# Down products of 768 tokens by a 2x2 recursion of seven, and attention values taken a turn later

## The chip, the cores and the metric

The kernel runs on one core of one Trainium2 chip. The metric is device microseconds from start to end of one execution, median of several. A second number, the span, is what the profiler saw from the first to the last instruction of one profiled execution. The engines are called PE (TensorE; its weight load is listed as PEld), DVE (VectorE), ACT (ScalarE), POOL (GpSimd) and SP (SyncE). SP and POOL issue most DMAs.

## The reference

One layer of a gated hybrid decoder for 1024 prompt tokens and 8 sample tokens (1032 in all), model width 1024, feed-forward width 2816 (22 blocks of 128):

```python
z = x @ w_in
a_out = rg_lru(conv4(xr)) * gelu(yr)                # branch a
s_out = sliding_window_attention(q, k, v, sinks)    # branch s: window 128, 16 heads, 4 kv heads, head_dim 64
c_out = mem_attn(xq, mem_k, mem_v)                  # branch c: 256 memory tokens
merged = sum(gates[:, :, n] * (br @ w_branch[n]) for n, br in enumerate((a_out, s_out, c_out)))
h = layer_norm(ALPHA * x + merged @ w_out, ln1_g, ln1_b)
gt, up = jnp.split(h @ w_gate_up, 2, axis=-1)
h = layer_norm(ALPHA * h + (jax.nn.silu(gt) * up) @ w_down, ln2_g, ln2_b)
```

Outputs are h for both groups, the new recurrent states and the new key and value caches; for the sample group the window cache moves by one position (copies named o_swk and o_swv).

## The kernel before, in words

Tensors lie transposed: features on the 128 partitions, tokens along the columns. Every fp32 product is made of three matmuls in a rounded type (mm3): each operand is split into a high part (a cast on ACT, line 81) and a low part (source minus high part, on DVE, line 82), and the product is high x high, high x low and low x high, summed in one PSUM bank. So each operand tile costs one ACT and one DVE operation, and each product needs both before its three matmuls can run.

Stages in order of time: the input projection (up to about 690 us), memory attention with parts of branches a and c (to 830), local attention (`windows`, 830 to 1040) with branch products between its steps, branch s and the output projection (to 1217), gate and up (to 1677), down with the second layer norm (to 1933), and the end of the last layer norm.

**Local attention.** 4 kv heads x 8 blocks of 128 tokens give 32 turns. A turn makes scores and a softmax for one block (`win_scores`: PE scores L590 and L591, DVE L594, ACT L598), then fills with branch matmuls (`fill(1)`), then finishes the block of the turn before (`win_values`: PE transposes L615 into a bank bt, ACT and DVE split it into bph and bpl, PE multiplies both with the values into a bank bo, L620 and L621).

**Gate and up.** 20 of the 22 blocks are units f = 2 to 21; gate and up of one block are products of 1024-wide rows made by a 2x2 recursion: seven products i = 0 to 6 in place of eight, over halves of the features and halves of the tokens. One unit step (f, i) is 24 matmuls of 258 columns (two column parts p). `fast_quarter` makes the weight operand of a step three steps ahead (a sum of weight quarters for i = 1, 2, 4, 5, then the split, u..h and u..l). After the products, DVE and ACT put the results together (za, zb, ft) and SP stores the silu(gt) * up row of the block to a DRAM scratch scr_f. In units 6 and 12, SP also copies a whole cache of 1 MB from DRAM to DRAM.

**Down.** `down` takes three chunks of tokens (CH: 384, 384, 264). Per chunk 22 rows are loaded by POOL from scr_f (L1260) and split (gh, gl), and for each of eight output blocks m, the weights are loaded by SP in pieces of up to 512 columns and split (wd_h, wd_l), so every weight piece is loaded and split three times over the stage; L1251 to L1253 are the three matmuls. The result of a block is added to the residual (L1307) and to a running sum (L1311). The layer norm of a chunk is a generator whose steps are taken between the products of the next chunk; the last chunk ends with a form of its own (`last_layer_norm`).

**Order.** The order on each engine is the order in which the code is written, as a recording layer puts it down with priorities; `issue_after` pins an operation behind a named one. Tiles come from pools; a pool opened after another has closed takes its room, and a tile waits for the last user of that room.

```python
def split(self, hi, lo, src):
    ins = self.nc.scalar.copy(hi, src).ins
    self.nc.vector.tensor_sub(lo, src, hi.bitcast(F32))
    return ins
```

## Time and profile before

| what | us |
|---|---|
| runs before, median of 3 | 1946.44 |
| lowest, highest | 1943.93, 1948.19 |
| time of the profiled execution | 1948.63 |
| its span | 1946.9 |
| mean granted TensorE clock | 0.996 |
| gate and up, main stretch | 1216.8 to 1655.0 |
| down, first to last matmul | 1677.7 to 1932.6 |

Rows of the views by stage give for each engine the busy time in a stretch and, in brackets, the instructions counted there. A granted clock of 1.00 means that TensorE was never slowed there. In rows of waits, the columns are the total time waited, how often, and the longest; the engine is named first, then what it wanted to write and at which line, and behind the arrow what it waited for. In groups by line, `out<-in` names the tiles, the shape is partitions x columns, and `319` is the mean duration in ns.

### The profile page before, as it was taken

The page shows a single profiled execution, that of the slowest core. Times are in us where ns is not written, and L with a number is a line of the kernel's source. Part 1 is how long each engine was busy: PE and PEld are TensorE (multiplying, and loading weights), DVE is VectorE, ACT ScalarE, POOL GpSimd, SP SyncE. Part 2 cuts the span into 40 slices and gives each one's busy share as a digit, 9 for nine tenths or more (in the row PEclk, how much of TensorE's full clock was granted, in tenths as well). Part 3 has the DMA queues.
Part 4 walks back from the last instruction along what each step waited for, and adds up shares of the span by engine and source line. Part 5 has one row for each costly group of instructions (what it writes and reads, how often), then busy time and mean ns, then how long its engine had stood idle before and what let it go on. Part 6 is the DMA issues. An engine that isn't in the chain of part 4 may idle for free. (4 is left out here: it accounts for less than half of the span.)

```text
span 1946.9 us, 37967 instructions
## 1 busy us (share of the span) xinstructions
PE 1912.7 (98%) x14356; PEld 1883.0 (97%) x14356; DVE 1363.5 (70%) x2875; ACT 1012.9 (52%) x2198; POOL 133.8 (7%) x218
## 2 busy tenths in 40 slices
PE   8999999999999999999999999999999999999997
PEld 8999999999999989989999999999999999999997
DVE  8678887888777645389877557975565656747566
ACT  5465565455556545388775245643333333635444
POOL 1000000000010200011110000000000000402002
PEclk9999999999999999999999999999999999999999
DMA  7444545465323866567525341122222222846554
GB/s 231 146 160 148 174 166 184 128 215 168 130 90 134 287 206 222 153 170 218 161 77 171 99 145 46 39 78 97 78 88 87 90 80 78 280 130 186 158 155 138
DMA packets 170919, 281.92 MB, mean 145 GB/s; under 512 B 20864, under 2 KB 85456, under 8 KB 170704
## 3 DMA queue, kind: packets, MB, share of 16 engines
q1 hardware_dynamic: 165840, 264.72, 43.2%
q0 software_dynamic: 4896, 14.78, 2.3%
q8 instruction: 112, 1.84, 0.4%
q14 instruction: 71, 0.58, 0.1%
HBM read 214.64 MB, written 66.85 MB: 145 GB/s over the span
## 5 line engine op out<-in xcount | busy, mean ns | idle before, releaser
L1253 PE MATMUL dl<-gh,wd_l 128*128 128x384 f32 (+1 forms) x528 | 168.5, 319 | 3.1 <-DVE wd_l L82 3.1
L1251 PE MATMUL dl<-gh,wd_h 128*128 128x384 f32 (+1 forms) x528 | 168.0, 319 | 1.1 <-ACT gh L81 1.1
L1252 PE MATMUL dl<-gl,wd_h 128*128 128x384 f32 (+1 forms) x528 | 168.2, 319 | 0.0
L1253 PEld LDWEIGHTS dl<-gh,wd_l 128*128 128x128 f32 x528 | 99.9, 189 | 3.5 <-DVE wd_l L82 3.5
L1251 PEld LDWEIGHTS dl<-gh,wd_h 128*128 128x128 f32 x528 | 99.9, 189 | 1.3 <-ACT gh L81 1.3
L1252 PEld LDWEIGHTS dl<-gl,wd_h 128*128 128x128 f32 x528 | 99.9, 189 | 0.5 <-DVE gl L82 0.5
L1260 POOL DMA_DIRECT2D gl<-scr_f x66 | 35.5, 539 | 789.0 <-PE fb L1186 630.6
L81 ACT CAST u_1h<-us 128x512 fp32r<-128x512 f32 x48 | 29.8, 621 | 87.2 <-issue 43.5
L598 ACT ACTIVATE bp<-bp,bst 128x257 f32<-128x257 f32 (+1 forms) x128 | 62.8, 493 | 18.1 <-DVE bst L594 18.0
L287 DVE TENSOR_TENSOR us<-ur,ur 128x512 f32<-128x512 f32 x96 | 66.0, 688 | 5.1 <-DMA ur<-win 3.1
L81 ACT CAST u_2h<-us 128x512 fp32r<-128x512 f32 x48 | 29.7, 619 | 76.6 <-PE fb L1186 38.2
L287 DVE TENSOR_TENSOR us<-us,ur 128x512 f32<-128x512 f32 x96 | 66.2, 689 | 2.3
L82 DVE TENSOR_TENSOR u_6l<-ur,u_6h 128x512 fp32r<-128x512 f32 x48 | 33.9, 706 | 44.9 <-PE fb L1187 28.9
L115 PE MATMUL brs<-bsH,wbs_h 128*128 128x384 f32 (+1 forms) x192 | 61.1, 319 | 1.0 <-ACT bsH L81 1.0
L82 DVE TENSOR_TENSOR u_4l<-us,u_4h 128x512 fp32r<-128x512 f32 x48 | 33.0, 688 | 40.1 <-PE fb L1187 29.1
L117 PE MATMUL brs<-bsH,wbs_l 128*128 128x384 f32 (+1 forms) x192 | 61.0, 318 | 0.0
L116 PE MATMUL brs<-bsL,wbs_h 128*128 128x384 f32 (+1 forms) x192 | 61.0, 318 | 0.0
L594 DVE CUSTOM_DVE_ANT_0 bp<-bs,mask,nsnk 128x256 f32<-128x256 f32 (+1 forms) x128 | 54.6, 458 | 3.2 <-PE bs L591 2.2
L82 DVE TENSOR_TENSOR u_5l<-us,u_5h 128x512 fp32r<-128x512 f32 x48 | 33.1, 689 | 30.0 <-PE fd L1187 14.9
L1205 ACT ACTIVATE ft<-za 128x516 f32<-128x516 f32 x40 | 25.5, 636 | 52.4 <-DVE za L1204 52.4
L81 ACT CAST u_5h<-us 128x512 fp32r<-128x512 f32 x48 | 30.0, 624 | 38.2 <-DVE us L287 24.9
L81 ACT CAST u_0h<-ur 128x512 fp32r<-128x512 f32 x48 | 29.8, 621 | 38.5 <-PE ub L304 19.1
(2019 smaller groups left out, 8111.4 us busy)
## 6 DMA issues: line engine op xcount, KB each, us to landing
ur<-win SPq DMA_DIRECT2D x112, 256.0 KB
ur<-wgu SPq DMA_DIRECT2D x80, 256.0 KB
scr_f<-ft SPq DMA_DIRECT2D x40, 258.0 KB
gl<-scr_f POOLq DMA_DIRECT2D x44, 192.0 KB, 4.3
dck<-cmk SPq DMA_DIRECT2D x32, 256.0 KB
dcv<-cmvT SPq DMA_DIRECT2D x32, 256.0 KB
st<-scr_q SPq DMA_DIRECT2D x32, 256.0 KB
scr_g<-za SPq DMA_DIRECT2D x10, 516.0 KB
```

What stands on the lines that cost most here:

```text
L81: ins = self.nc.scalar.copy(hi, src).ins
L82: self.nc.vector.tensor_sub(lo, src, hi.bitcast(F32))
L115: nc.tensor.matmul(ps, sh, mh, start=i == 0, stop=False)
L116: nc.tensor.matmul(ps, sh, ml, start=False, stop=False)
L117: self.last_mm = nc.tensor.matmul(ps, sl, mh, start=False, stop=closes and i == last).ins
L287: nc.vector.tensor_add(src, a, b)
L594: nc.vector.tensor_tensor_reduce(pg[g], s[:, u * 256:u * 256 + n], msk, 1.0, snk[:, g:g + 1], ALU.add, ALU.min, st[:, g:g + 1])
L598: nc.scalar.activation(x, x, AF.Exp, bias=st[:, g:g + 1], scale=-1.0, accum_out=st[:, 4 + g:5 + g])
L1251: nc.tensor.matmul(ps, sh, mh, start=k == 0, stop=False)
L1252: nc.tensor.matmul(ps, sh, ml, start=False, stop=False)
L1253: self.last_mm = nc.tensor.matmul(ps, sl, mh, start=False, stop=closes and k == NF - 1).ins
L1260: self.nc.gpsimd.dma_start(lo.bitcast(F32), self.scf[f][:, t0:t0 + n])
```

## The change

**Down.** The first 384 columns of each token half (768 tokens) go through the same recursion that gate and up use: seven products over halves of the 22 blocks (KD = 11), halves of the output blocks and the two token sides, taken in the order 0, 3, 2, 1, 5, 4, 6. A product is 4 output pairs j x 11 blocks k x 3 matmuls of 384 columns. The remaining 264 tokens (132 of each half) are taken the plain way at the end. Products 1, 2, 4 and 5 need sums of weight quarters, products 1, 2, 4 and 6 sums of row quarters.

**Where the sums are made.** 16 weight jobs in gate and up: POOL loads four pieces, four DVE additions, POOL stores four results to a DRAM scratch scr_w. Row sums per k: POOL loads two rows (two more are at hand), four DVE operations, four stores to scr_s; the last k comes in down (`last_sums`). The scratch tiles of both (pool xs) are four rooms.

**Kept lows.** The low parts of the weights of products 0, 3 and 6 stay in SBUF (wk tiles), so that three quarters of the weight pieces of the last 264 tokens need only the cast on ACT.

**Other parts.** The end of unit 21 (`unit_end`) is held until after down's first weights. The two 1 MB cache copies become sixteen. The halves of the tokens are now interleaved quarters, and a unit's row is stored in one contiguous piece. The layer norm of one token side lies in product 6, that of the other in the last part. In `windows` the transposes with their split (`win_turn`) and the value products (`win_values`) are separate, and the values of a block come one turn later, not before the sixth matmul of the branch product that fills the turn (`self.mark`). Widths of the chunks change from 384, 384, 264 to 384, 390, 258.

Local attention on PE, around the scores of block 3 of kv head 1 (bt are transposes, bs scores, bo values, bra and brc branch products). Before:

```order
L117 MATMUL bra7_2_11920<-H0_7h_8918,wba71_l_11762 128x264
L615 MATMUL bt1_1_0_11947<-ident_63,bp1_1_11823 128x128 x4
L615 MATMUL bt1_1_1_11958<-ident_63,bp1_1_11823 128x128 x4
L590 MATMUL bs1_3_0_11980<-ks1_0_11442,st1_0_11448 128x256
L591 MATMUL bs1_3_0_11980<-ks1_1_11443,st1_0_11448 128x256
L590 MATMUL bs1_3_0_11980<-ks1_0_11442,st1_1_11451 128x256
L591 MATMUL bs1_3_0_11980<-ks1_1_11443,st1_1_11451 128x256
L620 MATMUL bo1_1_11946<-bph1_1_0_11952,vs1_11460 128x512
L590 MATMUL bs1_3_1_11987<-ks1_0_11442,st1_2_11454 128x256
```

and now:

```order
L128 MATMUL bra7_2_11924<-H0_7h_8933,wba71_l_11764 128x258
L639 MATMUL bo1_0_11950<-bph1_0_0_11894,vs1_11462 128x512
L640 MATMUL bo1_0_11950<-bpl1_0_0_11895,vs1_11462 128x512
L626 MATMUL bt1_1_0_11961<-ident_63,bp1_1_11825 128x128 x4
L626 MATMUL bt1_1_1_11970<-ident_63,bp1_1_11825 128x128 x4
L601 MATMUL bs1_3_0_11982<-ks1_0_11444,st1_0_11450 128x256
L602 MATMUL bs1_3_0_11982<-ks1_1_11445,st1_0_11450 128x256
L601 MATMUL bs1_3_0_11982<-ks1_0_11444,st1_1_11453 128x256
```

The values of block 1 stood four score matmuls behind their own transposes; now the values of block 0 stand there, whose transposes were a turn earlier, ahead of the branch product.

DVE where the units end and down begins (ft21 is the last unit's row, gl the low part of a row of down, wd or wk the low part of weights). Before:

```order
L1206 SCALAR_TENSOR_TENSOR ft21_1_21655<-ft21_1_21655,za21_1_21654 128x516
L1209 SCALAR_TENSOR_TENSOR ft21_0_21639<-fb21_0_21521,ft21_0_21639 128x258
L1207 TENSOR_TENSOR ft21_1_21655<-ft21_1_21655,zb21_1_21683 128x258
L1209 SCALAR_TENSOR_TENSOR ft21_1_21655<-fb21_1_21536,ft21_1_21655 128x258
L82 TENSOR_TENSOR wd0_1_00_l_22008<-wd0_1_0r0__22005,wd0_1_00_h_22007 128x512
L82 TENSOR_TENSOR gl0_0_21840<-gl0_0_21840,gh0_0_21839 128x384
L82 TENSOR_TENSOR gl1_0_21845<-gl1_0_21845,gh1_0_21844 128x384
```

and now:

```order
L91 TENSOR_TENSOR gl0_7_22289<-gl0_7_22289,gh0_7_22288 128x384
L91 TENSOR_TENSOR wk0_1_0_22314<-wd0_1_0r_22311,wd0_1_0h_22313 128x512
L91 TENSOR_TENSOR wk0_1_1_22320<-wd0_1_1r_22317,wd0_1_1h_22319 128x512
L91 TENSOR_TENSOR wk0_1_2_22326<-wd0_1_2r_22323,wd0_1_2h_22325 128x384
L1236 SCALAR_TENSOR_TENSOR ft21_0_22071<-ft21_0_22071,za21_0_22070 128x516
L1236 SCALAR_TENSOR_TENSOR ft21_1_22087<-ft21_1_22087,za21_1_22086 128x516
L1237 TENSOR_TENSOR ft21_0_22071<-ft21_0_22071,zb21_0_22101 128x258
L1237 TENSOR_TENSOR ft21_1_22087<-ft21_1_22087,zb21_1_22115 128x258
L1239 SCALAR_TENSOR_TENSOR ft21_0_22071<-fb21_0_21945,ft21_0_22071 128x258
L1239 SCALAR_TENSOR_TENSOR ft21_1_22087<-fb21_1_21960,ft21_1_22087 128x258
L91 TENSOR_TENSOR gl0_8_22342<-gl0_8_22342,gh0_8_22341 128x384
```

The end of the last unit stood ahead of all row lows; now it stands behind eight of them and the lows of the second weights, ahead of the ninth row.

The diff, cut to its core (functions that vanish whole, `streamed` and `rows`, and the loaders of rows and weights are left out):

```diff
+CH = ((0, 384), (384, 390), (774, 258))
+CW = 390
-EARLY, EARLY_ROWS = ("mm", "s", "mm", "s"), 12
+KD = NF // 2
+NA = 384
+NC = T // 2 - NA
+DOWN_ORDER = (0, 3, 2, 1, 5, 4, 6)
+DOWN_PIECES = ((0, 4), (4, 4), (8, 3))
+SUM_PIECES = ((0, 3), (3, 3), (6, 3), (9, 2))
+KEPT = (0, 3, 6)
+EARLY = 4
+SUM_AT = {1: 0, 2: 1, 4: 2, 5: 3}
+ROW_AT = {1: 0, 4: 1, 2: 2, 6: 3}
...
+            if i == 2:
+                self.mark = self.last_mm
...
+    def win_turn(self, kv, ops, b, pg):
+
         nc = self.nc
-        nk, vs = len(range(max(b - 1, 0), b + 1)), ops[2]
-        ov = self.bank("o", f"bo{kv}_{b}")
-        for kk in range(nk):
+        out = []
+        for kk in range(2 if b else 1):
             pt = self.bank("t", f"bt{kv}_{b}_{kk}")
             for g in range(4):
                 nc.tensor.transpose(pt[:, g * P:(g + 1) * P], pg[g][:, kk * P:(kk + 1) * P], self.ident)
             hi = self.ph.tile([P, 512], F32R, tag="pt", name=f"bph{kv}_{b}_{kk}", bufs=4)
             lo = self.ph.tile([P, 512], F32R, tag="pt", name=f"bpl{kv}_{b}_{kk}", bufs=4)
             self.split(hi, lo, pt)
-            v = vs[:, max(b - 1, 0) + kk, :]
-            nc.tensor.matmul(ov, v, hi, start=kk == 0, stop=False)
-            self.last_mm = nc.tensor.matmul(ov, v, lo, start=False, stop=kk == nk - 1).ins
+            out.append((hi, lo))
+        return kv, ops[2], b, out
+
+    def win_values(self, kv, vs, b, pp):
+        nc = self.nc
+        ov = self.bank("o", f"bo{kv}_{b}")
+        with self.tc.issue_after(self.mark):
+            for kk, (hi, lo) in enumerate(pp):
+                v = vs[:, max(b - 1, 0) + kk, :]
+                nc.tensor.matmul(ov, v, hi, start=kk == 0, stop=False)
+                nc.tensor.matmul(ov, v, lo, start=False, stop=kk == len(pp) - 1)
...
-        nxt, last = self.win_load(0), None
+        nxt, last, turned = self.win_load(0), None, None
         fill(2)
         for kv in range(4):
             ops = nxt
                 pg = self.win_scores(kv, ops, b)
                 if last:
                     fill(1)
-                    self.win_values(*last)
+                if turned:
+                    self.win_values(*turned)
+                turned = last and self.win_turn(*last)
                 last = kv, ops, b, pg
                 if b == 4 and kv < 3:
                     nxt = self.win_load(kv + 1)
         fill(1)
-        self.win_values(*last)
+        self.win_values(*turned)
+        self.win_values(*self.win_turn(*last))
...
+            elif self.held is None:
+                self.unit_end(st, i, p, f, za, t, b, d)
             else:
+                self.held.append(partial(self.unit_end, st, i, p, f, za, t, b, d))
+
+    def unit_end(self, st, i, p, f, za, t, b, d):
+        nc, lo_, hi_ = self.nc, slice(0, QN), slice(QN, HT)
+        if i == 5:
+            nc.vector.tensor_add(za[:, hi_], d, st["s", 2, p])
+            nc.scalar.activation(t, za, AF.Tanh, scale=0.5)
+            nc.vector.scalar_tensor_tensor(t, t, 1.0, za, op0=ALU.add, op1=ALU.mult)
+            nc.vector.tensor_mul(t[:, hi_], t[:, hi_], st["zb", p])
+        else:
+            nc.vector.scalar_tensor_tensor(t[:, lo_], b, -0.5, t[:, lo_], op0=ALU.mult, op1=ALU.mult)
+            nc.sync.dma_start(self.scf[f][:, p * HT:(p + 1) * HT], t)
+
...
+    def scratch(self, name, n):
+        return self.xs.tile([P, NA], F32, tag="xs", name=name, bufs=4)[:, :n]
+
+    def sum_load(self, j, e):
+
+        o, n = SUM_PIECES[e][0] * P, SUM_PIECES[e][1] * P
+        raw = [self.scratch(f"dw{j}{e}{x}", n) for x in range(4)]
+        for x, a in enumerate(raw):
+            at = (x % 2) * KD * P + o
+            self.nc.gpsimd.dma_start(a, self.io["wdn"][2 * j + x // 2][:, at:at + n])
+        return j, o, n, raw
+
+    def sum_weights(self, j, o, n, raw):
+
+        nc, (a11, a12, a21, a22) = self.nc, raw
+        with self.tc.issue_after(self.last_mm):
+            nc.vector.tensor_add(a22, a21, a22)
+            nc.vector.tensor_add(a21, a11, a21)
+            nc.vector.tensor_add(a11, a22, a11)
+            nc.vector.tensor_add(a12, a11, a12)
+        for i, a in ((1, a22), (4, a21), (2, a11), (5, a12)):
+            nc.gpsimd.dma_start(self.scw[j][:, SUM_AT[i], o:o + n], a)
+
+    def row_load(self, k):
+        x = [self.scratch(f"rx{k}{h}", NA) for h in range(2)]
+        for h in range(2):
+            self.nc.gpsimd.dma_start(x[h], self.scf[k][:, h * HT:h * HT + NA])
+        return x
+
+    def row_sums(self, k, x00, x01, x10, x11, t1, t4, queue):
+
+        nc = self.nc
+        nc.vector.tensor_sub(t1, x00, x01)
+        nc.vector.tensor_sub(x01, x11, x01)
+        nc.vector.scalar_tensor_tensor(x00, x01, -1.0, x00, op0=ALU.mult, op1=ALU.subtract)
+        nc.vector.scalar_tensor_tensor(t4, x00, -1.0, x10, op0=ALU.mult, op1=ALU.subtract)
+        for i, a in ((1, t1), (4, x01), (2, x00), (6, t4)):
+            queue.dma_start(self.scs[k][:, ROW_AT[i] * NA:(ROW_AT[i] + 1) * NA], a)
...
+        jobs = deque((j, e) for j in range(KT // 2) for e in range(len(SUM_PIECES)))
...
-            if (f, i) in ((6, 2), (12, 2)):
-                name, cache = ("o_swk", "cwk") if f == 6 else ("o_swv", "cwv")
+            if i == 2 and f > 3 and caches:
+                name, cache, b = caches.popleft()
                 with self.tc.issue_after(self.last_load):
-                    self.nc.sync.dma_start(io[name][:, 0:P - 1, :], io[cache][:, 1:P, :])
+                    self.nc.sync.dma_start(io[name][b, 0:P - 1, :], io[cache][b, 1:P, :])
             if n + ahead < len(todo):
                 v, j = todo[n + ahead]
                 self.fast_quarter(st[v], j)
+            if (f, i) == (NF - 1, 5):
+                self.held = []
             self.unit_step(st[f], i)
+            if n % 4 == 0 and jobs:
+                job = self.sum_load(*jobs.popleft())
+            elif n % 4 == 3 and job:
+                self.sum_weights(*job)
+                job = None
+            if i == 3 and KD <= f < NF - 1:
+                early = self.row_load(f - KD)
+            if i == 1 and turn:
+                with self.tc.issue_after(self.last_mm):
+                    self.row_sums(*turn, self.nc.sync if f == NF - 1 else self.nc.gpsimd)
+                turn = None
             if i == 6:
+                if KD <= f < NF - 1:
+                    k = f - KD
+                    turn = (k, *early, *(st[f]["t", p][:, :NA] for p in range(2)),
+                            *(self.scratch(f"rs{k}{x}", NA) for x in range(2)))
                 del st[f]
...
+    def down_begin(self):
+        self.norm, self.lows = None, {}
+        self.rooms()
+        first = partial(self.down_row, DOWN_ORDER[0])
+        self.first_rows = [first(k, "a") for k in range(8)]
+        self.first_weights = {(DOWN_ORDER[0], 0, e): self.down_weights(DOWN_ORDER[0], 0, e) for e in range(3)}
+        with self.tc.issue_after(self.row_cast):
+            self.first_weights.update({(DOWN_ORDER[0], 1, e): self.down_weights(DOWN_ORDER[0], 1, e) for e in range(3)})
+            for held in self.held:
+                held()
+        self.first_rows += [first(k, "a") for k in range(8, KD)]
...
+        for n, i in enumerate(DOWN_ORDER):
+            ahead = deque(range(KD))
+            nxt = [None] * KD
+            for j in range(KT // 2):
+                opens = i in (0, 1, 3)
+                if opens:
+                    tag = ("mm", "mm", "mm", "o")[j] if i == 0 else "st"[j % 2]
+                    banks["b" if i == 0 else "c", j] = self.bank(tag, f"dl{i}_{j}")[:, :NA]
+                ps = banks["b" if i in (0, 2, 4, 6) else "c", j]
+                mm = partial(nc.tensor.matmul, ps, skip_group_check=not opens)
+                for e, (k0, nk) in enumerate(DOWN_PIECES):
+                    wh, wl = self.weights_of(i, j, e)
+                    for k in range(k0, k0 + nk):
+                        w = slice((k - k0) * P, (k - k0 + 1) * P)
+                        xh, xl = act[k]
+                        mm(wh[:, w], xh, start=opens and k == 0, stop=False)
+                        mm(wh[:, w], xl, start=False, stop=False)
+                        self.last_mm = mm(wl[:, w], xh, start=False, stop=k == KD - 1).ins
+                    if ahead:
+                        k = ahead.popleft()
+                        if i == 6:
+                            last[k] = self.last_row(k)
+                        else:
+                            nxt[k] = self.down_row(DOWN_ORDER[n + 1], k, "ba"[n % 2])
+                    if i == 6 and (j, e) in ((2, 0), (2, 2), (3, 1)):
+                        self.norm_step()
+                evict(i, j, ps)
+            act = nxt
+            if i == 0:
+                self.last_sums()
+            if i == 4:
+                norm_of(1)
+        for f in range(KD, NF):
+            last[f] = self.last_row(f)
...
+        for m in range(EARLY):
+            open_[m] = self.bank(("mm", "s")[m % 2], f"dc{m}")[:, :2 * NC]
+            half(m, 0, open_[m], False)
+            self.norm_step()
+            if m == EARLY - 2:
+                norm_of(0)
```

More of the change, by code (lines that the diff above doesn't have):

```diff
@@ L1314, in build @@
+        tail = lambda a: a.rearrange("p (q n) -> p q n", q=2)
+        rows = [tail(a)[:, :, NA:] for a in self.accs]
+        self.last_layer_norm(2 * NC, rows, product, V_G2, emit_to(lambda m: tail(io["o_y"][:, m, :])[:, :, NA:]), tail)
     def build(self):
@@ L1341, in build @@
                         held()
+                self.held = None
             self.sums = 2
```

263 lines of the change are left out of this document (159 added, 104 removed).

## The prediction

> **What bounds the kernel now.** The page's first part comes first: one engine fills the span.
>
> ```profile
> span 1946.9 us, 37967 instructions
> PE 1912.7 (98%) x14356; PEld 1883.0 (97%) x14356; DVE 1363.5 (70%) x2875; ACT 1012.9 (52%) x2198; POOL 133.8 (7%) x218
> PE 13%; DVE 0%; ACT 0%; issue 0%; ACTq 0%; DVEq 0%
> ```
>
> PE is busy for 98%, and the chain that ended last (third line) is followed back through PE for 13% of the span, which is the whole down stage. So time goes away only where matmuls go away or where PE stands still. Second view: busy time by stage (columns: stretch, length, then PE, PEld, DVE, ACT, POOL, granted clock, DMA share, GB/s).
>
> ```profile
> 1216.80:1655.00 438.20, 436.93 (x3644) 436.36 (x3643) 288.14 (x550) 180.81 (x365) 0.00 (x0) 1.00 0.25 80
> 1655.00:1677.60 22.60, 21.61 (x181) 21.40 (x179) 13.00 (x26) 8.91 (x19) 11.36 (x21) 1.00 0.83 265
> 1703.50:1752.20 48.70, 48.70 (x283) 48.70 (x282) 23.25 (x41) 15.29 (x27) 0.00 (x0) 1.00 0.47 130
> 1677.66:1862.20 184.54, 184.54 (x1062) 184.04 (x1063) 115.39 (x216) 90.55 (x181) 24.19 (x45) 1.00 0.59 177
> 1862.20:1932.60 70.40, 67.35 (x539) 66.72 (x539) 50.83 (x92) 36.87 (x71) 5.85 (x6) 0.98 0.54 160
> 1932.60:1946.90 14.30, 2.33 (x13) 1.66 (x11) 7.60 (x14) 5.69 (x12) 3.91 (x5) 0.71 0.22 76
> 830.00:1040.00 210.00, 207.20 (x1337) 191.77 (x1337) 175.26 (x541) 162.50 (x488) 37.58 (x61) 1.00 0.53 148
> ```
>
> Gate and up (1216.8 to 1677.6) runs a matmul of 258 columns every 436.36/3643 = 0.120 us; PE hardly waits, DVE has 34% of the time free and ACT 59%. In down the undisturbed stretch 1703.5 to 1752.2 gives one of 384 columns each 48.70/283 = 0.172 us. Local attention (830 to 1040) is tighter: DVE 83%, ACT 77%. Third view: what PE's weight load waits for in local attention, then what its matmuls wait for in the whole run.
>
> ```profile
> PEld bo L620 <- ACT bph L81: 7.0, 25, 0.5
> PEld bo L620 <- PE bra L116: 0.7, 1, 0.7
> PEld bo L620 <- issue: 0.5, 2, 0.3
> PE dl L1253 <- DVE wd_l L82: 3.1, 2, 2.2
> PE fb L1187 <- DVE u_0l L82: 1.3, 2, 0.6
> PE dl L1251 <- ACT gh L81: 1.1, 1, 1.1
> ```
>
> Value matmuls lose 8.2 us to the cast of the probabilities just transposed; down loses 1.1 us at its start and 3.1 us near its end; the units lose 1.3 us in two places.
>
> **The change, part by part.** The sum is made on the profiled execution, 1948.6 us around its span of 1946.9; the median of the runs is 1946.4, 2.2 lower, and that is taken off at the end.
>
> *Fewer matmuls: -22.7.* For 768 tokens the plain product takes 2 x 8 x 22 x 3 = 1056 matmuls of 384 columns, the recursion 7 x 4 x 11 x 3 = 924. 132 x 0.172 = 22.7 us. The other 264 tokens stay 528 matmuls. Chunks of 390 and 258 columns in place of 384 and 264 keep the columns of the earlier stages the same: nothing.
>
> *Values a turn later: -7.5.* The value matmuls now stand behind a whole fill of branch matmuls, and their operands were cast a turn before, so the 8.2 us lose their cause. What is left is how much of it comes back as a wait of the scores or transposes, on engines at 83% and 77%. Bounds: 0, all of it comes back, and -10, if smaller waits around it go too. I stay near the row, -7.5.
>
> *Cache copies: -1.3.* Two copies of 1 MB were queued ahead of a unit's weights; the two waits for u_0l are 1.3 us, the longest 0.6. Sixteen small copies, each in another unit, should leave none. Bounds -1.3 and 0.
>
> *The sums in the units: 0.* 16 weight jobs of four adds and 11 row jobs of four operations (one in down) are about 108 DVE instructions. The nearest rows are the 384-wide ones:
>
> ```profile
> L82 DVE TENSOR_TENSOR gl<-gl,gh 128x384 fp32r<-128x384 f32 x44 | 21.9, 555 | 2.6 <-ACT gh L81 2.6
> L1307 DVE SCALAR_TENSOR_TENSOR acc<-acc,dl 128x384 f32<-128x384 f32 x16 | 8.8, 552 | 4.3 <-PE dl L1253 4.3
> L981 DVE RECIPROCAL n2rs<-n2rs 128x384 f32<-128x384 f32 x2 | 5.1, 2554 | 0.7 <-ACT n2rs L978 0.7
> L1206 DVE SCALAR_TENSOR_TENSOR ft<-ft,za 128x516 f32<-128x516 f32 x3 | 2.1, 694 | 0.7 <-ACT ft L1205 0.7
> L1209 DVE SCALAR_TENSOR_TENSOR ft<-fb,ft 128x258 f32<-128x258 f32 x4 | 1.7, 425 | 0.0
> L82 DVE TENSOR_TENSOR gl<-gl,gh 128x264 fp32r<-128x264 f32 x22 | 8.8, 429 | 3.4 <-ACT gh L81 3.3
> L287 DVE TENSOR_TENSOR us<-ur,ur 128x512 f32<-128x512 f32 x96 | 66.0, 688 | 5.1 <-DMA ur<-win 3.1
> ```
>
> 104 x 0.55 = 57 us in a stage with 150 us of free DVE: 66% becomes 79%. What hides them is PE's own pace; uncovered they would cost 57 us, and the place where cover can fail is the third rival. The units' traffic, 80 GB/s, grows by some 11.5 MB of weight loads, 3.9 MB of row loads and 19 MB of stores in 438 us, to about 160 GB/s; the stretch before down ran at 265.
>
> *Units into down: +4.7.* In the new order DVE does, after the unit's last sums, three weight lows, eight row lows (gl0_0 to gl0_7), then three lows of the next weights (wk0_1, 2 x 0.69 + 0.555 = 1.9 us), then the held end of unit 21 (2 x 0.694 + 2 x 0.42 + 2 x 0.425 = 3.1 us), and only then gl0_8. PE goes through 24 matmuls on gl0_0 to gl0_7 for the first quarter and eight on the second before it needs gl0_8: about 32 x 0.172 = 5.5 us. From DVE's first row low, gl0_8 is ready after 9 x 0.555 + 1.9 + 3.1 = 10.0 us, and PE starts some 0.5 us after that low. So PE stands still for 9.5 - 5.4 = about 4.2 us. After such a stop the clock drops, as two places show, each behind a PE gap (the 2.2 us of the wd_l row above, and 1.8 us at 716):
>
> ```profile
> 716.00:721.00 5.00, 4.79 (x23) 4.79 (x24) 1.48 (x4) 1.02 (x4) 0.54 (x3) 0.66 0.46 139
> 1880.00:1885.00 5.00, 4.23 (x22) 4.23 (x23) 4.03 (x8) 1.01 (x3) 0.00 (x0) 0.66 0.56 159
> PEld dss L887 <- POOL dsk L884: 1.8, 1, 1.8
> ```
>
> A granted clock of 0.66 over 5 us is 3.4 us at half speed: 1.7 us of work lost. Together 5.9, less the 1.1 to 1.3 that the old start lost: +4.7. Bounds 0 (the rows land so late that the held work fits in before them) and +8 (the rows land at intervals and gl0_8's own landing comes on top).
>
> The Trainium skill, "TensorE: Matmul & The Clock Gate", Part 1, says that the clock falls to half after at least one idle window of about 3.4 us. The two gaps above are shorter and were followed by a half-speed window all the same, so here the measurement decides. By the page the 4.2 us stop would still pay, but a stop of 2 us would not: its sum would be up to 1.7 us lower if my stop is overestimated.
>
> *The steady products: 0.* One product takes PE 132 x 0.172 = 22.7 us. DVE does twelve weight lows (8 x 0.69 + 4 x 0.555 = 7.7), eleven row lows (6.1), four evictions (2.2) and at most four running sums (2.2): 18.2 us. POOL issues eleven row loads, SP twelve weight loads: 2.1 MB + 2.9 MB in 22.7 us, 220 GB/s, where 265 was reached.
>
> *The last part: 0.* 528 x 0.120 x 264/258 = 65 us of PE against 70.4 in the row above, so the old one lost some 5 us (3.1 of wd_l, and a slow window). The new one has weight lows for a quarter of its pieces only (the others are kept), but two layer norms instead of one now lie in the last product and in it, each with a reciprocal of 2.55 us in front of weight lows that PE waits for. I put stalls of 4 to 6 us there: 0, with bounds -4 and +2. The tail of 14.3 us has the same operations.
>
> Sum: -22.7 - 7.5 - 1.3 + 0 + 4.7 + 0 + 0 = -26.8; 1948.6 - 26.8 = 1921.8 on the profiled scale, less 2.2: **1919.5 us**.
>
> **The rivals.**
>
> *DVE becomes the bound in down.* For it: the first product has, beside 18.2, the last row sums (2.2), its own eleven row lows (6.1) and the held work (3.1), less 1.9 done before it starts: 27.7 us against 22.7; product 6 has weight lows 7.7, eleven row lows of 0.43, evictions 4.4 and a norm of 8 x 0.55 + 7 x 0.55 + 2.55 + 8 x 0.61 + 1.1 = 16.8, together 33.6 against 22.7. Against it: the norm is cut into steps that may slide into the last part, where DVE has room. If neither slides, 5.0 + 10.9 come in full, 15.9; some 6 of it are in my sum already (the stop at the start), so about 10 more: 1929.5.
>
> *The windows gain nothing:* 83% and 77% are already the pace of DVE and ACT, the freed 7.5 us reappear before the scores or the transposes. Against it: in the rows above the wait falls on one instruction 25 times, 0.28 us each, and PE is the fullest engine. 1927.
>
> *Slower: the ring of four rooms for the weight sums.* One job loads four pieces on POOL, DVE adds four times, POOL stores four, and the next job's loads wait for these stores. DVE's adds stand in its one queue ahead of the lows of the next unit steps, so when a load is late, PE starves.
>
> ```profile
> L1260 POOL DMA_DIRECT2D gl<-scr_f x66 | 35.5, 539 | 789.0 <-PE fb L1186 630.6
> DMA to landing us min/median/max: 2.6/4.0/6.5
> ```
>
> With L from issue to landing, one turn of the ring is 4 x 0.55 + 2 x 0.54 + 2L = 3.3 + 2L. Four unit steps are 96 x 0.120 = 11.5 us. At the median 4.0 it fits (11.3); from 4.1 on each of 16 jobs falls behind, 3 steps (8.6 us) of splits made ahead absorb the first of it, and from L = 5.2 on 16 x (3.3 + 2L - 11.5) - 8.6 is over 27 and the kernel is slower than before; at 6.5 it is 16 x 4.8 - 8.6 = 68 us, about 1987. For it: the median is near the edge. Against it: these landings were measured with DMA 59 to 83% busy, the units have 25%. The Trainium skill, "DMA: Bandwidth & Descriptors", Anatomy of one DMA, fits about 2.0 us plus the bytes at 436 GB/s for this path: an estimate of 2.45 us for 192 KB and a turn of 8.2 us, well hidden. The fastest row, 2.6, agrees; the median does not.
>
> *No stalls at all:* the start has its cover, the last part loses its 5 us: -22.7 - 8.2 - 1.3 - 1.2 - 4 = 37, 1909.
>
> **How the numbers follow.** Forecast 0.58, DVE-bound 0.18, windows nothing 0.12, ring 0.08, no stalls 0.04. The forecast's own range, from its bounds, is 1912 to 1926; the other two faster cases and the no-stall one take it to 1909 and 1934 (DVE-bound with its upper price). Outside lies the ring and a little of each. A measurement of this kernel tells 0.2%, about 4 us, from no change: all cases but the ring are faster by more (0.92); of the ring 0.02 ends near no change and 0.06 slower.
>
> **What would show it.** Down: 924 matmuls of 384 columns and 0.172 us each, from the first to the last one some 22 us less than before. Start: one PE wait of about 4 us on the low of gl0_8 and a clock below 1.00 behind it. Windows: the row of bo waiting for bph is gone and 830 to 1040 is 7 to 8 us shorter. Units: the same 2.88 us a step, with DVE near 79%; PE waits there for u lows, with POOL loads landing after 4.1 us, would mean the ring. Last part: waits for weight lows behind the reciprocal. I am wrong if a matmul of the recursion takes longer than 0.172, if gl0_8 is no wait, or if down's DVE stands at 95% over several products.

## The result, and the profile after

The changed kernel takes 1967.17 us (median of 4 runs, 1964.38 to 1967.92), the kernel before 1946.76 (4 runs): a ratio of 1.0106, 95% interval 1.0092 to 1.0119. It is slower by 20 us where 1919.5 was predicted. Its profiled execution took 1967.92 us with a span of 1966.1.

The page of the changed kernel, first part:

```profile
span 1966.1 us, 38210 instructions
PE 1901.7 (97%) x14224; PEld 1874.0 (95%) x14224; DVE 1402.8 (71%) x2980; ACT 1024.3 (52%) x2219; POOL 257.4 (13%) x435
```

PE has 132 matmuls less and 11 us less work, and yet the span is 19 us longer. The stages tell where. Columns as before: stretch, length, busy PE, PEld, DVE, ACT, POOL, granted clock, DMA share, GB/s. First the changed kernel: local attention, units, two parts of the units, down of the 768 tokens, last part.

```profile
826.00:1040.70 214.70, 210.00 (x1376) 198.16 (x1375) 176.89 (x545) 169.80 (x492) 38.14 (x61) 0.99 0.56 153
1271.00:1712.20 441.20, 415.37 (x3363) 413.44 (x3362) 293.67 (x566) 152.62 (x310) 108.24 (x199) 0.97 0.50 161
1300.00:1480.00 180.00, 154.66 (x1187) 153.00 (x1187) 110.77 (x220) 50.98 (x107) 61.44 (x113) 0.91 0.57 183
1480.00:1712.20 232.20, 232.20 (x1943) 232.20 (x1943) 158.68 (x302) 89.14 (x178) 36.96 (x68) 1.00 0.43 140
1712.20:1876.90 164.70, 161.55 (x928) 160.23 (x927) 119.09 (x232) 85.66 (x175) 44.14 (x77) 1.00 0.73 229
1877.00:1951.30 74.30, 68.58 (x545) 67.51 (x544) 42.39 (x83) 46.76 (x94) 10.00 (x13) 0.98 0.61 186
```

and the same four stages of the kernel before, cut at the same operations:

```profile
826.70:1043.60 216.90, 213.10 (x1378) 197.46 (x1376) 177.94 (x546) 164.24 (x492) 37.58 (x61) 1.00 0.55 152
1272.30:1677.70 405.40, 403.07 (x3363) 402.46 (x3361) 247.28 (x465) 153.15 (x306) 11.36 (x21) 1.00 0.30 95
1677.70:1862.20 184.50, 184.50 (x1062) 184.00 (x1063) 115.35 (x215) 90.51 (x181) 24.19 (x45) 1.00 0.59 177
1862.20:1932.90 70.70, 67.65 (x542) 67.02 (x542) 50.83 (x92) 36.87 (x71) 5.85 (x6) 0.98 0.54 159
```

Down of the 768 tokens gives 19.8 us; local attention 2.2; the last part costs 3.6. The units cost 35.8 us, nearly all of it between 1300 and 1480, where the weight sums are made: there PE is idle for 25 of 180 us and the granted clock is 0.91. After 1480, where the row sums are made and the weight sums are done, PE has no idle time at all. In the units PE's busy time grew as well, 415.4 for 403.1 us with the same 3363 matmuls: that is the slow clock behind the stops. What the weight load waits for, in the changed kernel:

```profile
PEld fb L1208 <- DVE ft L1239: 26.0, 8, 6.1
PEld n2va1p L978 <- ACT n2va1h L90: 3.5, 1, 3.5
PEld dl L1471 <- DVE ft L1239: 2.8, 1, 2.8
PEld n2va0p L978 <- ACT n2va0h L90: 1.7, 1, 1.7
```

The largest is new: eight waits of the bank fb for ft, the last operation of the unit before. One of them on DVE, in order of time (start, duration, idle time before and its releaser):

```profile
1410.21 0.68 DVE L91 TENSOR_TENSOR u_1l<-us,u_1h 128x512 fp32r<-128x512 f32 x1
1415.42 0.43 DVE L1258 TENSOR_TENSOR dw<-dw,dw 128x256 f32<-128x256 f32 x1 [4.53 <-DMA dw<-wdn]
...
1416.37 0.42 DVE L1234 TENSOR_TENSOR za<-fd,u2s 128x258 f32<-128x258 f32 x1
...
1419.98 0.42 DVE L1239 SCALAR_TENSOR_TENSOR ft<-fb,ft 128x258 f32<-128x258 f32 x1
```

and on POOL and PE in the same stretch:

```profile
1408.76 0.54 POOL L1263 DMA_DIRECT2D scr_w<-dw  x1 [0.52 <-DVE za L1222]
1409.33 1.22 POOL L1251 DMA_DIRECT2D dw<-wdn  x2
1411.53 0.55 POOL L1251 DMA_DIRECT2D dw<-wdn  x1 [0.98 <-DMA scr_w<-dw]
1412.80 0.54 POOL L1251 DMA_DIRECT2D dw<-wdn  x1 [0.73 <-DMA scr_w<-dw]
1420.45 0.58 PE L1208 MATMUL fb<-H_0h,u_0h 128*128 128x258 f32 x1 [5.85 <-DVE ft L1239]
```

DVE is done at 1410.9, but the next thing in its queue is an addition of a weight job whose last piece was issued only at 1412.8, when a store of the job before had landed and freed its room. DVE stands 4.5 us. Behind it are the za and ft operations that end the unit; ft (1419.98 to 1420.4) reads the bank in which PE wants to start the next unit's second column part, and PE stands 5.85 us. DVE's idle time in front of L1258 is 48.4 us in all, by the groups of its lines:

```profile
L1258 DVE TENSOR_TENSOR dw<-dw,dw 128x384 f32<-128x384 f32 x12 | 6.7, 559 | 31.9 <-DMA dw<-wdn 31.6 <-issue 0.3
L1258 DVE TENSOR_TENSOR dw<-dw,dw 128x256 f32<-128x256 f32 x4 | 1.7, 427 | 16.7 <-DMA dw<-wdn 16.7
dw<-wdn POOLq DMA_DIRECT2D x48, 192.0 KB, 3.3
scr_w<-dw POOLq DMA_DIRECT2D x48, 192.0 KB, 2.9
```

The last two rows are the landings in that stage: 3.3 us for loads and 2.9 for stores, shorter than the median of 4.0 that the prediction took for its ring.

### The profile page after: what moved, and what is told of

Read it like the earlier page. It is cut to its first block, busy times and chain, and to the rows that moved or that the text cites. A ratio compares the mean times of both kernels' runs of the same rounds, so it can differ in the third digit from the quotient of the medians.

```text
span 1966.1 us, 38210 instructions
## 1 busy us (share of the span) xinstructions
PE 1901.7 (97%) x14224; PEld 1874.0 (95%) x14224; DVE 1402.8 (71%) x2980; ACT 1024.3 (52%) x2219; POOL 257.4 (13%) x435
## 5 line engine op out<-in xcount | busy, mean ns | idle before, releaser
L1251 POOL DMA_DIRECT2D dw<-wdn x64 | 34.8, 543 | 299.5 <-DVE h_3l L91 250.6
L126 PE MATMUL brs<-bsH,wbs_h 128*128 128x384 f32 (+2 forms) x192 | 61.1, 319 | 1.0 <-ACT bsH L90 1.0
L127 PE MATMUL brs<-bsL,wbs_h 128*128 128x384 f32 (+2 forms) x192 | 61.1, 319 | 0.3 <-DVE bsL L91 0.3
L128 PE MATMUL brs<-bsH,wbs_l 128*128 128x384 f32 (+2 forms) x192 | 61.3, 320 | 0.0
L797 POOL TENSOR_SCALAR tr<-th 128x1032 f32<-128x1032 f32 x8 | 11.0, 1374 | 313.8 <-DVE sq L796 156.9
L91 DVE TENSOR_TENSOR gl<-gl,gh 128x384 fp32r<-128x384 f32 x77 | 39.8, 552 | 15.6 <-ACT gh L90 15.5
L616 POOL TENSOR_SCALAR bp<-bp,bst 128x256 f32<-128x256 f32 (+1 forms) x32 | 32.1, 1002 | 134.8 <-DVE bst L610 134.8
L90 ACT CAST gh<-gl 128x384 fp32r<-128x384 f32 x77 | 36.5, 511 | 21.9 <-DMA gl<-scr_s 14.8
L91 DVE TENSOR_TENSOR bpl<-bt,bph 128x512 fp32r<-128x512 f32 x60 | 41.0, 686 | 7.0 <-ACT bph L90 6.3
L1473 PE MATMUL dl<-gh,wk 128*128 128x384 f32 x132 | 44.2, 336 | 0.6 <-DVE wk L91 0.6
```

Source lines behind the costliest of these rows:

```text
L126: nc.tensor.matmul(ps, sh, mh, start=i == 0, stop=False)
L127: nc.tensor.matmul(ps, sh, ml, start=False, stop=False)
L128: self.last_mm = nc.tensor.matmul(ps, sl, mh, start=False, stop=closes and i == last).ins
L616: (nc.gpsimd if g else nc.vector).tensor_scalar_mul(pg[g], pg[g], r)
L1251: self.nc.gpsimd.dma_start(a, self.io["wdn"][2 * j + x // 2][:, at:at + n])
L1473: self.last_mm = mm(wl[:, w], xh, start=False, stop=k == KD - 1).ins
```

## The experiments

Theory A: a POOL load that is late holds an addition, the addition holds DVE's one queue, and the end of the unit behind it holds PE's bank. Against it stand theory B, the added traffic delays the units' own weights; C, the pace of the ring alone; D, DVE's added work as such; E, the place in the queue alone.

### The additions left out

```diff
-            nc.vector.tensor_add(a22, a21, a22)
-            nc.vector.tensor_add(a21, a11, a21)
-            nc.vector.tensor_add(a11, a22, a11)
-            nc.vector.tensor_add(a12, a11, a12)
+            pass
```

> The change with the 64 additions of the weight jobs left out: the same loads from and stores to DRAM by POOL, the sums that are stored are raw pieces. Theory A (DVE's queue: the additions wait for a load that waits for the store of the job before, and the end of the unit, which frees PE's bank, stands behind them): the waits of fb for ft (26.0 us in the changed kernel) fall under 2 us, the granted clock stays at 1.00 from 1271 on to the start of down, the stage from the first fb to the first dl takes 405 to 408 us instead of 441, the whole 1930 to 1934 us. Theory B (the 35 MB of added traffic delay the units' own weights): the stage stays at 435 us or more, the whole at 1960 or more.

1960.89 us (one run), far from A's number and near B's. But the loss is not what B describes: nearly all of it is a single wait of PE.

```profile
PEld fb L1208 <- DVE zb L1225: 33.4, 1, 33.4
1396.36 0.56 DVE L1271 TENSOR_TENSOR rs<-rx,rx 128x384 f32<-128x384 f32 x1 [40.46 <-DMA rx<-scr_f]
1392.96 1.12 POOL L1265 DMA_DIRECT2D rx<-scr_f  x2
1268.70:1366.00 97.30, 97.30 (x815) 97.24 (x814) 57.14 (x106) 37.12 (x75) 50.60 (x94) 1.00 0.75 252
```

The first row is a wait, the second and third DVE's and POOL's timeline, the fourth a stretch of the units before the stop. DVE stood 40 us for the first operation of the first row sum, L1271. The code puts it after step 1 of unit 12, with `issue_after(self.last_mm)`, and it ran in the middle of unit 6: the named instruction is one of PE, and it held back nothing on DVE, where the row sum came to stand six units early. Why the recording layer chose that place isn't shown. Its load stood on POOL behind the jobs not yet done, which take 6.5 us each. So it is the same chain once more, with another DVE operation. In the 97 us before, DMA was at 0.75 and 252 GB/s without any wait of PE, which speaks against B.

### Again, with the row sums pinned to a DVE operation

```diff
-                with self.tc.issue_after(self.last_mm):
+                with self.tc.issue_after(self.pin):
```

Here `self.pin` is the last DVE operation of the unit before (ft, L1239).

> Once more without the 64 additions of the weight jobs (raw pieces are stored), now with the row sums pinned in DVE's order behind the last operation of the unit before; in the first such run one of them had come to stand in unit 6, behind six weight jobs in POOL's queue, and held DVE and PE for 33.4 us. Theory A (only a DVE operation ahead of the unit's end that waits for a POOL load stops PE): no PE wait over 1 us and a clock of 1.00 in the units, 404 to 406 us from the first fb to the first dl, the whole 1926 to 1930 us. Theory B (traffic): the same DMA as in the change, so waits of fb for u lows of some 10 us or more, 415 us or more, the whole above 1937.

1926.13 us (one run), and the units take 402.1 us with PE busy for all of it, at 53% DMA and 176 GB/s:

```profile
1265.70:1667.80 402.10, 402.10 (x3362) 402.05 (x3361) 265.63 (x502) 156.39 (x310) 107.78 (x199) 1.00 0.53 176
```

B is out: all loads and stores of the change are there, and PE waits for nothing. Compared with 441.2 this also gives the price of the fault: 39.1 us, of which 441.2 - 415.4 = 25.8 are PE's idle time and 415.4 - 402.1 = 13.3 the slow clock.

### The additions at another place in DVE's queue

Jobs are added up behind the last ft of a unit (L1239) and behind za of step 3 (L1222), the two operations that `self.pin` names in turn; everything else stays.

```diff
-            if n % 4 == 0 and jobs:
-                job = self.sum_load(*jobs.popleft())
-            elif n % 4 == 3 and job:
+            if i in (0, 3) and job:
                 self.sum_weights(*job)
                 job = None
+            elif i in (1, 4) and jobs:
+                job = self.sum_load(*jobs.popleft())
...
-        with self.tc.issue_after(self.last_mm):
+        with self.tc.issue_after(self.pin):
             nc.vector.tensor_add(a22, a21, a22)
```

> The change with all additions, loads and stores of the weight jobs and the same four rooms, but the additions pinned in DVE's order: one job behind the last operation of a unit, one behind the za operations of step 3; so two jobs a unit, one every 3.5 steps (10.1 us) instead of 4 (11.5 us). Theory A (it is the place in DVE's queue, ahead of the unit's end, that turns a late load into a PE wait): fb waits under 5 us, units 405 to 412 us, the whole 1930 to 1938 us. Theory C (it is the pace: a turn of the ring takes about 9.9 us and any job that finds it late costs PE the difference, wherever it stands): with the faster pace the fb waits stay at 25 us or grow, the whole 1965 or more. Theory D (57 us of additional DVE work as such): unchanged, 1960 to 1970.

1937.47 us (4 runs), 0.9959 of before, interval 0.9946 to 0.9973: faster than before, and 30 us faster than the change, with all its work. So C and D fall: the same work on DVE, its jobs 10.8 us apart on the mean where the change had 12.0 (with its stops), and PE's waits for ft and zb went from 27.7 to 8.4 us. In steps the pace is the same: in the order that came out, the change too had two jobs to a unit. What differs is the place.

```profile
PEld fb L1208 <- DVE ft L1239: 6.6, 5, 1.6
PEld fb L1208 <- DVE zb L1225: 1.8, 2, 1.1
1268.00:1679.80 411.80, 404.41 (x3362) 402.61 (x3361) 293.92 (x566) 151.42 (x310) 107.72 (x199) 1.00 0.52 172
```

```profile
L1258 DVE TENSOR_TENSOR dw<-dw,dw 128x384 f32<-128x384 f32 x12 | 6.7, 559 | 28.2 <-DMA dw<-wdn 24.1 <-issue 4.1
```

DVE still stands 28 us in front of the wide additions, where it stood 32 in the change (5 for 17 in front of the narrow ones), up to 4 us at a time, so many loads are still late; at their new place most of it costs PE nothing. The stage takes 411.8 us, at the upper end of what A expected.

### The same place, with loads that are early

```diff
-            if n % 4 == 0 and jobs:
+            if i == 4 and job:
+                self.sum_weights(*job)
+                job = None
+            if i == 4 and f < 10:
                 job = self.sum_load(*jobs.popleft())
-            elif n % 4 == 3 and job:
-                self.sum_weights(*job)
-                job = None
...
```

The additions are pinned behind zb of step 4 (L1225), and so are the row sums.

> The additions stand pinned at the place where the change has most of its waits, between zb of step 4 and the end of the unit, but one job a unit, loaded seven steps (20.2 us) ahead. Eight of the sixteen jobs are made so (units 3 to 10); for the other eight, raw pieces are copied from DRAM to DRAM in units 12 to 19 in place of sums. Theory A, first half (a load that is late): no wait of PE over 1 us in units 3 to 10. Theory E (the place alone costs, 2.2 us of additions ahead of the unit's end while PE has one step, 2.9 us, to spare): a wait of 1 to 3 us in each of these eight units. The whole kernel's time is of no interest here (copies).

```profile
1265.60:1667.70 402.10, 402.10 (x3362) 402.04 (x3361) 278.39 (x534) 154.76 (x310) 73.31 (x135) 1.00 0.45 148
```

One run, with half of the jobs, one to a unit. PE has no wait in the units, to the last digit the 402.1 of the run without additions. E falls: additions right ahead of the unit's end cost nothing when their data are there. It takes both, the late load and the place.

### Stores of the sums by SP

```diff
-            nc.gpsimd.dma_start(self.scw[j][:, SUM_AT[i], o:o + n], a)
+            nc.sync.dma_start(self.scw[j][:, SUM_AT[i], o:o + n], a)
```

> As the pinned kernel, with the stores of the weight sums issued by SP instead of POOL and the row sums pinned too. In the pinned kernel the job in the middle of a unit still comes 3.1 us late (its turn: additions 2.9, four stores and four loads on POOL 5.1, landing 3.8 us against 10.1), and fb waits 8.4 us. If the turn decides, SP's issue takes 2.2 us out of it: fb waits under 5 us, units 406 to 409 us, 2 to 5 us less than the pinned kernel's 1937. Rival (SP's stores wait for additions and delay the units' weights queued behind them): u lows wait for their loads, units 412 us or more.

1926.93 us (4 runs), 0.9912 of before, interval 0.9897 to 0.9927; 10.5 us less than with POOL's stores, more than expected. The units, and below them the part of the pinned kernel's units in which its row sums lie:

```profile
1267.30:1671.50 404.20, 402.63 (x3362) 402.16 (x3361) 294.31 (x566) 154.13 (x310) 72.91 (x135) 1.00 0.53 176
1460.00:1679.80 219.80, 219.80 (x1839) 219.80 (x1839) 150.01 (x285) 84.67 (x170) 36.77 (x68) 1.00 0.44 144
```

404.2, 7.6 us less than the pinned kernel's 411.8, is 2 us from the floor of 402.1. The row sums are pinned in this kernel too, but where they lie the pinned kernel had no idle time on PE (second row), so the gain is that of the stores. With four stores less in POOL's queue the loads come earlier: DVE waits 7.8 us for them in front of the additions (17.1 in the trace of a later kernel with the same units) where it waited 29.2. The profiled spans differ by 10.9 us, of which down gave 1.4 and the last part 1.2; neither was changed, and their clock was 0.99 and 0.95 in the pinned kernel, 1.00 and 0.98 here.

### The start of down and the norm

```diff
-            tag = ("mm", "mm", "mm", "o")[j] if i == 0 else "st"[j % 2]
+            tag = ("mm", "o", "mm", "mm")[j] if i == 0 else "st"[j % 2]
...
         self.first_weights = {(DOWN_ORDER[0], 0, e): self.down_weights(DOWN_ORDER[0], 0, e) for e in range(3)}
+        self.first_rows += [first(k, "a") for k in range(8, KD)]
         with self.tc.issue_after(self.row_cast):
...
                 held()
-        self.first_rows += [first(k, "a") for k in range(8, KD)]
...
-                    if i == 6 and (j, e) in ((2, 0), (2, 2), (3, 1)):
+                    if i == 6 and (j, e) in ((2, 0), (2, 2)):
...
-            if m in NORM_AT:
+            if m in (0, 2, 3, 4):
```

> As the pinned kernel, and two edits in down. Start: the last three rows of the first product are split before the held end of unit 21, and the second output pair starts in the bank o instead of one that the held operations free. Norm: the variance matmul of the first side one step later (in the last part), that of the second side one product later. If the traces of the changed kernel are read rightly, the wait of dl for ft (2.8 us) and those of n2va1p and n2va0p (3.5 and 1.7) go, with the slow clock behind the second: 6 to 9 us less than the pinned kernel. Rival (DVE is simply behind there and the wait moves to the next low that PE needs): within 2 us of the pinned kernel.

1928.73 us (4 runs), 0.9923 of before, interval 0.9909 to 0.9936. By the medians that is 8.7 us less than the pinned kernel, inside the 6 to 9 expected; but the profiled execution, the slowest of the four at 1933.41, shows only 3.6 of them: down took 162.7 us for 166.0, and the last part 74.3 for 74.6. So in this trace the start paid and the norm didn't: the variance waits fell from 3.4 and 1.8 us to 0.9, and another wait stands in their place.

```profile
PEld dc L1499 <- ACT wl_0h L1393: 4.8, 1, 4.8
PEld n2va1p L978 <- ACT n2va1h L90: 0.9, 1, 0.9
```

The start alone, on top of SP's stores:

> Pinned additions and row sums, stores of weight sums by SP, and the edit of the start alone. In the run without it the first PE wait of down was 2.8 us, for the held ft that frees the bank; with it 0 to 1.2 us (for a low of wk): 1.6 to 2.8 us less than 1926.9. Rival: gl0_8 or the next lows take its place, no change.

1924.49 us (4 runs), 0.9891, interval 0.9878 to 0.9905: 2.4 us less than without, as expected, though the intervals overlap. Down went from 164.6 to 162.3 us, and the wait of dl for ft is gone. Over all traces down takes 162.3 to 163.0 us in the four kernels with this edit and 164.2 to 167.1 in the six without it, so this gain is clear.

### All edits, and the rows of the last part later

```diff
-        for f in range(KD, NF):
-            last[f] = self.last_row(f)
+        open_, behind = {}, deque(range(KD, NF))
...
                 wh, wl = self.last_weights(m, kh, e)
+                if behind and (m, e) != (0, 0):
+                    f = behind.popleft()
+                    last[f] = self.last_row(f)
```

> Pinned additions and row sums, stores of weight sums by SP, the edits of start and norm, and the last eleven rows of the plain part loaded piece by piece in the first halves of the last part instead of all ahead of it. In the run with start and norm edits the wait had moved: dc for wl_0h 4.8 us, with ACT's casts of those rows, each waiting for its landing, standing ahead of the cast of the weights. If that is the cause, dc's waits fall under 2 us and the slow clock of 6.8 us there goes: last part 67 to 70 us instead of 74.3; with the units as in the run above, 1916 to 1922 us. Rival (another wait takes its place, the norm's reciprocal in front of weight lows): last part 72 to 74, the whole 1924 to 1927.

1924.29 us (4 runs), 0.9898, interval 0.9881 to 0.9914; the last part took 75.1 us, so the rival is right: the wait for wl_0h fell from 4.8 to 1.7 us, and waits for lows took its place. The last edit takes the blocks with kept lows first:

```diff
-        for m in range(EARLY):
+        for at_, m in enumerate((0, 2, 1, 3)):
```

> As the kernel with all edits (1924.3), with the first halves of the last part taken in the order 0, 2, 1, 3: blocks 0 and 2 have kept lows and need nothing of DVE while it ends the norm. If DVE's reciprocal in front of the lows (waits for wl_0l 1.9 and wl_1l 3.3 us) is what holds the last part, it falls from 75 to 70 or 71 us and the whole to 1919 to 1921. Rival (ACT's casts of rows and weights hold it as much): 73 to 75 us, 1923 to 1925.

1928.39 us (6 runs), 0.9915, interval 0.99 to 0.993, last part 75.5 us: not shorter, and the whole is above both expectations. The last part isn't why: in the profiled executions the first fb comes at 1270.5 us here and at 1265.1 in the run before, after stages whose code is the same. Differences of a few us between single executions say little in this series. The waits of the two runs, the first with all edits, the second in the other order:

```profile
PEld dc L1501 <- DVE wl_1l L91: 3.3, 1, 3.3
PEld dc L1501 <- DVE wl_0l L91: 1.9, 2, 1.3
PEld dc L1499 <- ACT wl_0h L1393: 1.7, 1, 1.7
```

```profile
PEld dc L1501 <- DVE wl_0l L91: 4.1, 2, 3.7
PEld dc L1499 <- ACT wl_0h L90: 1.9, 1, 1.9
```

Four arrangements, and the last part stays between 73 and 76 us, with 5 to 8 us of waits that only change their name. What sets it wasn't found. DVE is busy there for 42 to 43 us and ACT for 47 of 75, so neither is full over the stage as a whole.

### Local attention alone

The kernel before with `win_turn`, the new `win_values` and `windows`, nothing else.

> The kernel before with the change of local attention alone (values a turn later). My prediction's step: 7.5 us less, 1939. What the two traces suggest (216.8 to 214.7 us from the first scores to branch s): 2 us less, 1944.7, within what the measurement can tell. Rival: a loss of up to 2 us, since the transposes now wait (bt 1.6 to 4.0 us).

1940.24 us (8 runs), 0.9979 of before, interval 0.9968 to 0.999: 4 us less by the ratio, between the two numbers. The stage, and two of the waits in front of the transposes:

```profile
822.70:1035.30 212.60, 208.20 (x1376) 196.00 (x1375) 176.92 (x545) 169.10 (x492) 37.68 (x61) 1.00 0.55 153
PEld bt L617 <- ACT bp L605: 1.3, 3, 0.7
PEld bt L617 <- DVE bpl L82: 0.7, 2, 0.4
```

It gives 4.3 us of 216.9. The 7.0 us of bo for bph are gone; the waits of bt, 1.5 us in the kernel before, are 3.4 now, so 2 of the 7 came back in front of the transposes.

## Why the prediction was wrong, step by step

**"The sums in the units: 0"** is the step that failed: +35.8 us. It counted DVE's free time (150 us for 57 of work) and PE's pace, and both were right: pinned and with SP's stores the same additions run in 402.3 to 406.6 us, in four executions of the same code. These are the longest and the shortest:

```profile
1268.20:1674.80 406.60, 403.61 (x3363) 402.49 (x3362) 294.03 (x566) 154.15 (x313) 73.12 (x135) 1.00 0.52 174
1270.50:1672.80 402.30, 402.30 (x3362) 402.14 (x3361) 294.50 (x566) 156.06 (x313) 72.91 (x135) 1.00 0.53 176
```

Free time says how much work fits in, not whether a queue may stand still. What the runs showed in place of the 0 is a wait: DVE stood 48 us for late loads of these sums, PE stood 25.8 us behind it for the bank that the unit's end frees, and the slow clock after these stops took 13.3 us more.

**The rival of the ring** had the first half of the chain, at 0.08, and wrote it off by two wrong conditions.

One: it took four steps, 11.5 us, from one job's additions to the next, as the code is written. On DVE the trace has two jobs to a unit, most of them one between u_5l and u_6l and one behind u_1l, directly ahead of the unit's end: three and four steps apart in turn. Nothing on DVE held them to their step, as the row sum of the first experiment shows for the same hint. Three steps (8.6 us) are shorter than the ring's turn, which took 9.9 us in the stretch shown above (starts at 1405.54 and 1415.42).

Two: it allowed 8.6 us of slack, since weight lows are made three steps ahead. The end of a unit stands in the same queue and has no such lead: PE needs ft's bank half a unit step after the next unit begins.

The third term, the turn 3.3 + 2L, was right: with the landings measured it is 3.3 + 3.3 + 2.9 = 9.5 us for the 9.9. By the rival's own rule (a loss from L = 5.2 on) the kernel would have been faster, and its sign, waits for u lows with landings after 4.1 us, did not come: PE waited for ft. The estimate of 2.45 us by the Trainium skill, "DMA: Bandwidth & Descriptors", Anatomy of one DMA, was low: the landings were 3.3 and 2.9. It would have changed nothing, since the turn was not what failed. (Two slips of arithmetic change nothing either: 9.5 - 5.4 is 4.1, and the ring's loss at L = 5.2 is 26.6 us, not over 27.)

**Fewer matmuls: -22.7.** Right. Without stops down of the 768 tokens is 924 x 0.172 = 158.9 us; it took 164.7 in the changed kernel and 162.3 to 167.1 over all runs, with its waits.

**Units into down: +4.7.** A stop of 2.8 us in place of 4.2, near the place named, but for another reason, and no slow clock behind it in this execution. It comes after 25 matmuls, not after 32, and the next matmul is the first on wd_0h of the second output pair:

```profile
1716.37 0.44 PE L1471 MATMUL dl<-gh,wd_2h 128*128 128x384 f32 x1
1719.35 0.44 PE L1471 MATMUL dl<-gh,wd_0h 128*128 128x384 f32 x1 [2.54 <-DVE ft L1239]
1711.57 3.83 DVE L91 TENSOR_TENSOR gl<-gl,gh 128x384 fp32r<-128x384 f32 x8
1718.88 0.75 DVE L1239 SCALAR_TENSOR_TENSOR ft<-fb,ft 128x258 f32<-128x258 f32 x2
```

Its bank is one that unit 21 still held, until the first held ft. I had followed the operands of the matmul and not its bank; with another bank (the edit of the start) the wait went. The third row is one reason why the stop is shorter too: eight lows in 3.83 us, where the prediction's 0.555 each make 4.4.

**Values a turn later: -7.5.** Too much; 4.3 us alone, 2.2 in this execution, where the stage's clock was 0.99, and 2.0 to 4.3 over the eleven traces with it. All lie inside the bounds, 0 and -10, that were kept for it. Of the 8.2 us in the three rows only 7.0 were a wait for the cast, and 2 of them came back before the transposes. **Cache copies: -1.3.** No wait for u_0l is left in any of these runs; not tried alone.

**The last part: 0.** +3.6, outside the bounds of -4 and +2. The reciprocal ahead of the lows was named; the variance matmul, which stands in PE's order ahead of its sum, was not, and removing it showed that more than one thing is late there. **Widths of chunks: nothing.** From branch s to gate and up the stage went from 182.7 us to between 184.6 and 184.8 in every run with the new widths, and stayed at 183.1 where only local attention was changed: some +1.5 to 2 that I had not counted. That it is the widths, and not the interleaved quarters that came with them, isn't shown.

**DVE as the bound in down** (0.18) did not come: DVE is busy for 119 of 164.7 us. Only in the first product was it full, 21.98 of 22.7 us.

With the additions and row sums pinned and the stores on SP the kernel takes 1926.9 us where 1919.5 was forecast, just outside the forecast's own range of 1912 to 1926; with the start's edit, which the prediction did not have, 1924.5. Both beat the kernel before.

## What to carry to other kernels

When work is added to an engine with free time, ask of each added instruction what it waits for and what stands behind it in the queue, and give the load in front of it the whole worst distance, not the mean pace. The ordering hint of this kernel holds only the engine of the instruction that it names; read the order that came out, on the engine that matters. For a matmul follow its bank as well as its operands: who reads it last, and what does that one wait for.

## What the hardware showed that was not expected

DVE's operations overlapped here. Eight lows of 128x384 that last 555 ns each ran in 3.83 us (row above): one starts every 0.47 us. Sums of mean durations, as in the prediction, are some 15% too high for such a run.

The clock after a stop depends on more than its length. The same stop of 2.8 us at the start of down left the clock at 1.00 in the changed kernel and brought a slow window in the pinned one (first and second row). Six traces have this stop: in four the clock stays at 1.00 over these 8 us, in the other two it is 0.79 and 0.65.

```profile
1716.00:1724.00 8.00, 5.46 (x31) 5.03 (x31) 8.00 (x18) 6.63 (x16) 0.83 (x2) 1.00 0.98 360
1684.00:1692.00 8.00, 5.43 (x21) 5.17 (x21) 7.40 (x17) 5.23 (x12) 0.81 (x2) 0.79 0.93 338
```

The Trainium skill, "TensorE: Matmul & The Clock Gate", Part 1, says that the window is free-running, so that it matters where in it the work falls; these two rows are compatible with that, and no run here shows where the window stood. Its threshold of one idle window of about 3.4 us is not what the stops here show, since 2.8 us was enough in the second row and 1.8 us at 716 in the kernel before.
